# An FFN down-projection by seven block products instead of eight, placed between the next group's up tiles, with the block sums on the vector engine

## The chip, the cores and the metric

The kernel runs on one core of a Trainium2 chip. The metric is the device time of one execution in microseconds, the median of several runs. Engines are named as in the profile: PE is the matrix engine (TensorE) and PEld its weight loads, DVE the vector engine, ACT the scalar engine, POOL is GpSimd, SP the engine whose queue starts the DMAs here.

## The reference, cut to what matters

One decoder layer on 256 tokens of 2048 channels, all in float32. The part that the change touches is the FFN at its end:

```python
h = rmsnorm(x, g_ffn[l])
u = causal_dwconv(h @ w_up[l], ffn_conv_w[l]) + ffn_conv_b[l]
gate, val = jnp.split(u, 2, axis=-1)
x = x + (jax.nn.silu(gate) * val) @ w_down[l]
return rmsnorm(x, g_final)
```

`w_up` is 2048 x 11264 (5632 gate and 5632 value channels), `w_down` is 5632 x 2048. Ahead of it stand a mixing block (projections, a gated convolution, pooling, cross-attention, an output projection), which the change leaves alone.

## The kernel before

All large products are made on PE from float32 numbers that are split in two parts: `hi`, the number rounded to the float32r format by an ACT copy (L129), and `lo`, the rest, by a DVE subtraction (L130). A product a x w is then hi x hi + hi x lo + lo x hi, three matmuls where one would do.

The weights come as one stream of tiles of 1 MB, in a fixed order (`stream`, L103). `load` puts the DMA of a tile on SP's queue into one of three `raw` buffers; `split_tile` makes its `hi` and `lo`, 2048 columns wide, into three buffers each; `next_tile` hands the tile to the product that uses it, and first has the tile three further on loaded and the one two further on split. The order of instructions on each engine is set by a scheduler from the order of the code; each engine then works its queue strictly in that order.

The FFN works on units of 256 channels, 22 in all. A unit has four up tiles: two halves of the 2048 input channels for the gate, two for the value (`unit_a`, `mm_a`: 32 matmuls a tile, 16 of 512 and 16 of 256 columns). When the gate's or the value's two tiles are through, `up_finish` (L737) takes the result from PSUM: per 128 channels an ACT copy of the correction (L322), two DVE operations (L323 the sum, L324 the norm's factor), an ACT operation (L747) and two DVE multiply-adds (L751) for the convolution, and for the gate ACT's Silu (L755). At the end of a unit DVE multiplies gate and value (L776), and ACT and DVE split the product (L777, L778) into a group's activation tile `u`.

Units are taken in groups of 8, 7, 5 and 2. A group's down-projection (`down`, L782) comes after the first unit of the next group, and those of the last two groups after all units. It goes through the group's chunks of 128 channels in tiles of two chunks x 1024 columns (`mm_b`, L326): 24 matmuls of 512 columns a tile, accumulated over the group in four PSUM banks, which DVE at last adds into the residual `xt` (`add_in`, L706). The last group (`down_last`, L793) goes by pieces, with the final norm between them.

Of the kernel before, what the change touches and what calls it, by code (L numbers as in the profile page):

```python
# [12 lines left out]
ALU = mybir.AluOpType  # L13
# [11 lines left out]
def kernel(  # L25
# [45 lines left out]
    # Per-channel vectors, as columns of 128 channels, by transposing rows of 128.  # L71
# [20 lines left out]
    rows = lambda v: v.rearrange("(r c) -> r c", c=P)  # noqa: E731  # L92
# [10 lines left out]
    stream = []  # (source, nk, ncol, pieces)  # L103
# [4 lines left out]
    def load(i, between=None):  # L108
        src, nk, ncol, pieces = stream[i]
        raw = wpool.tile([P, nk, ncol], F32, tag="raw", name=f"raw_{i}")  # L110
# [23 lines left out]
    def split_tile(i):  # L134
        nk, pieces = stream[i][1], stream[i][3]
        step = nk // pieces
# [19 lines left out]
    n_units = NF // 2  # L156
    UNITS = [8, 7, n_units - 17, 2]  # sizes of FFN groups in units of 256 channels
# [20 lines left out]
    # The pool's weights: per pair of groups the three chunks' rows, in the columns of  # L178
    # the output chunks that they reach; wp_at[k] is the first of them.
# [17 lines left out]
    # Chunks of the mix in the order in which they come about.  # L197
# [10 lines left out]
    # A group's down-projection comes after the next group's first unit; that of the  # L208
    # last but one after all units.
    sched = []  # L210
    done = 0
    for gi, (a, n) in enumerate(group_of):
        upto = n_units if gi + 2 >= len(group_of) else a + n + 1
        for u in range(done, upto):
            sched.append(("up", u, [g for g, (b, m) in enumerate(group_of) if b <= u][-1]))
        done = upto
        sched.append(("down", gi, None))
    for what, a, b in sched:
        if what == "up" and a == 0:
            for h in (0, 1):  # L220
                plan_a(w_up, 0, (h,))
                plan_a(w_up, D_UP, (h,))
        elif what == "up":
            plan_a(w_up, a * 256)
            plan_a(w_up, D_UP + a * 256)
        else:
            a0, n = group_of[a]
            for n2 in range(2):
                plan_b(w_down, a0 * 2, n * 2, n2 * 1024, 1024, 2)

# [27 lines left out]
    def rstd_of(ssq, nm):  # L258
        """ssq [P, n] sums of squares -> 1 / sqrt(mean + eps), with a Newton step."""
# [14 lines left out]
    def row_of(r, nm):  # L274
        """[P, TB] per-token values -> the same row of S values in every partition."""
# [44 lines left out]
    def gather(ps, row, o, engine=nc.vector):  # L320
        """(main + corrections) * row -> o [P, S] in SBUF."""
# [4 lines left out]
    def mm_b(ps, wt, actT, ks, tbs, first, last):  # L326
        """ps[tb][n] += act[tokens of tb, chunk k] @ w[chunk k, columns of n]."""
# [41 lines left out]
    # The order of the first instructions is that in which the data arrive.  # L369
# [66 lines left out]
    def split_into(o, src, n=S):  # L436
        """float32 [P, n] -> o, its two parts one after the other."""
# [50 lines left out]
    # 1 / (number of tokens averaged) for the first tokens  # L488
# [73 lines left out]
    # The sums run on GpSimd while the next unit's products do; the rest comes after.  # L562
    pending = []

    def pool_sums(ps, i):
# [3 lines left out]
        spans = []  # (first row, last row, group) of this chunk  # L569
# [17 lines left out]
    def pool_means():  # L587
        for i, v, spans, sums in pending:
# [11 lines left out]
            # The convolution's chunks of the mix are free until it comes.  # L600
# [122 lines left out]
    row_2 = None  # L723
    u_tiles = {}

    def up_matmul(u):
        if u:
            return [unit_a(h2T, f"g{u}"), unit_a(h2T, f"v{u}")]
        ps = [[bank(f"pu0_{w}_{mi}") for mi in range(2)] for w in range(2)]
        for h in range(2):  # L730
            for w in range(2):
                mm_a(ps[w], next_tile(), h2T, h * 8, 8, h == 0, h == 1)
                if h == 0 and w == 0:
                    transpose_in(xt, h2T, "g_ffn", range(8, 16), "x2")
        return ps
# [190 lines left out]
```

## Time and profile before

| | |
|---|---|
| time, median of 3 runs | 1064.57 us (1064.54 to 1064.72) |
| the profiled execution: its span | 1064.7 us |
| PE busy | 1054.7 us (99%) |
| DVE busy | 703.6 us (66%) |
| ACT busy | 529.0 us (50%) |
| instructions on PE | 5632 matmuls, as many weight loads |
| instructions on DVE | 920 |
| mean granted clock of TensorE | 0.997 |
| read from memory | 198.99 MB, 189 GB/s |

The profiled execution's own time is its span, within 0.15 us of each of the three runs. A row of a group reads: line, engine, operation, output <- inputs with their sizes, count | busy us, mean ns of one | idle time of the engine before them and what ended it. A row of a timeline reads: start, length, engine, line and operation, count, and in brackets the idle time before it with what ended that. Lengths of neighbours on one engine can overlap. Matmuls are pipelined, so that a busy PE alone does not say that it is at its peak; the chain of waits is the better witness.

### The profile page before, as it was taken

Reading aid. Unit: us, or ns where it says so; the run is one execution under the profiler, and the core shown is the slowest. Engines: PE = TensorE matmul, PEld = TensorE weight load, DVE = VectorE, ACT = ScalarE, POOL = GpSimd, SP = SyncE. Lnnn points to the kernel's source line nnn. Section 1 sums busy time; section 2 is a strip of 40 time slices with the busy share of each in tenths; the row PEclk is TensorE's granted clock in tenths of the full one; section 3 lists DMA queues with packets and bytes.
Section 4 is the critical chain, followed back from the end, with each engine's and each line's share of the span. In section 5 each row is a group of like instructions: output and inputs, shape, how many; then the busy total and the mean of one; then the engine's idle time right before and its main releaser. Section 6 shows DMA issues by size and latency. Waiting matters only on the chain.

```text
span 1064.7 us, 14249 instructions
## 1 busy us (share of the span) xinstructions
PE 1054.7 (99%) x5632; PEld 907.2 (85%) x5632; DVE 703.6 (66%) x920; ACT 529.0 (50%) x683; POOL 43.1 (4%) x163
## 2 busy tenths in 40 slices
PE   9999999999999999999999999999999999999996
PEld 8888898888888888888888888888888888888885
DVE  5677786764556777777744467777754477777655
ACT  5965454443446655555533344554533345555343
POOL 0023500000000000000000000000000000000000
PEclk9999999999999999999999999999999999999998
DMA  9765465455555556555555555655555555654552
GB/s 316 243 224 172 143 206 189 161 195 183 186 185 174 184 196 198 188 181 185 198 198 198 196 171 187 198 185 175 195 198 197 191 174 190 198 177 178 198 198 80
DMA packets 147342, 202.01 MB, mean 190 GB/s; under 512 B 3619, under 2 KB 125771, under 8 KB 147147
## 3 DMA queue, kind: packets, MB, share of 16 engines
q1 hardware_dynamic: 147242, 201.09, 55.8%
q8 instruction: 44, 0.72, 0.3%
q14 instruction: 24, 0.19, 0.0%
q10 hardware_dynamic: 32, 0.01, 0.0%
HBM read 198.99 MB, written 2.10 MB: 189 GB/s over the span
## 4 chain that ended last, share of the span: by engine, by line
PE 98%; DVE 1%; ACT 0%; issue 0%; DVEq 0%
PE pa_v L306 15%; PE pa_g L306 15%; PE pa_g L309 7%; PE pa_v L309 7%; PE pd L338 7%; PE pd L344 7%; PE pd L341 7%; PE po L338 3%; PE po L341 3%; PE po L344 3%; PE pa_cc L306 2%; PE pa_cx L306 2%; PE pa_cb L306 2%; PE pa_pv L306 2%; PE pk L395 2%; PE pa_q L306 1%
## 5 line engine op out<-in xcount | busy, mean ns | idle before, releaser
L130 DVE TENSOR_TENSOR lo<-raw,hi 128x2048 fp32r<-128x2048 f32 (+2 forms) x196 | 425.5, 2172 | 271.6 <-ACT hi L129 270.6
L129 ACT ACTIVATE hi<-raw 128x2048 fp32r<-128x2048 f32 (+2 forms) x196 | 355.9, 1818 | 255.8 <-PE pd L344 98.4
L306 PE MATMUL pa_v<-h2T,hi 128*128 128x512 f32 x672 | 236.7, 396 | 0.0
L306 PE MATMUL pa_g<-h2T,hi 128*128 128x512 f32 x672 | 236.7, 396 | 0.0
L309 PE MATMUL pa_g<-h2T,lo 128*128 128x256 f32 x672 | 188.5, 281 | 0.0
L309 PE MATMUL pa_v<-h2T,lo 128*128 128x256 f32 x672 | 188.5, 281 | 0.0
L306 PEld LDWEIGHTS pa_v<-h2T,hi 128*128 128x128 f32 x672 | 126.0, 188 | 30.0
L306 PEld LDWEIGHTS pa_g<-h2T,hi 128*128 128x128 f32 x672 | 126.0, 188 | 30.0
L309 PEld LDWEIGHTS pa_g<-h2T,lo 128*128 128x128 f32 x672 | 127.0, 189 | 0.1
L309 PEld LDWEIGHTS pa_v<-h2T,lo 128*128 128x128 f32 x672 | 127.0, 189 | 0.0
L338 PE MATMUL pd<-hi,u 128*128 128x512 f32 x320 | 98.6, 389 | 0.0
L341 PE MATMUL pd<-lo,u 128*128 128x512 f32 x320 | 98.5, 389 | 0.0
L344 PE MATMUL pd<-hi,u 128*128 128x512 f32 x320 | 98.5, 389 | 0.0
L751 DVE SCALAR_TENSOR_TENSOR t<-h,cols,t 128x256 f32<-128x256 f32 x176 | 79.1, 480 | 2.2 <-ACT t L747 1.4
L755 ACT ACTIVATE t<-t 128x256 f32<-128x256 f32 x44 | 18.3, 418 | 107.0 <-DVE t L751 107.0
L341 PEld LDWEIGHTS pd<-lo,u 128*128 128x128 f32 x320 | 60.1, 188 | 12.6
L344 PEld LDWEIGHTS pd<-hi,u 128*128 128x128 f32 x320 | 60.1, 188 | 12.4
L338 PEld LDWEIGHTS pd<-hi,u 128*128 128x128 f32 x320 | 59.9, 188 | 12.4
L747 ACT ACTIVATE t<-h,cols 128x256 f32<-128x256 f32 x88 | 49.8, 593 | 0.0
L322 ACT ACTIVATE h<-pa_g 128x256 f32<-128x256 f32 x42 | 16.0, 380 | 61.3 <-PE pa_g L309 61.3
L338 PE MATMUL po<-hi,mixT 128*128 128x512 f32 x128 | 39.6, 391 | 0.0
L341 PE MATMUL po<-lo,mixT 128*128 128x512 f32 x128 | 39.5, 389 | 0.0
(207 smaller groups left out, 1280.9 us busy)
## 6 DMA issues: line engine op xcount, KB each, us to landing
raw<-in_w_up_dram SPq DMA_DIRECT2D x88, 1024.0 KB, 5.0
raw<-in_w_down_dram SPq DMA_DIRECT2D x44, 1024.0 KB, 4.9
raw<-in_w_in_dram SPq DMA_DIRECT2D x28, 1024.0 KB, 4.9
raw<-in_w_out_dram SPq DMA_DIRECT2D x16, 1024.0 KB, 4.9
raw<-in_w_kv_dram SPq DMA_DIRECT2D x4, 1024.0 KB, 5.2
raw<-in_w_kv_dram SPq DMA_DIRECT2D x6, 512.0 KB, 8.3
memt<-in_mem_dram SPq DMA_DIRECT2D x8, 256.0 KB, 7.7
xt<-in_x_dram SPq DMA_DIRECT2D x4, 512.0 KB, 6.7
```

The source lines that it names most:

```text
L129: nc.scalar.activation(hi[:, s, :], raw[:, s, :], AF.Copy)
L130: nc.vector.tensor_tensor(lo[:, s, :], raw[:, s, :], hi[:, s, :].bitcast(F32), op=ALU.subtract)
L306: nc.tensor.matmul(ps[mi], hi[:, kk, c], actT[:, k, :], start=first and kk == 0, stop=False)
L309: nc.tensor.matmul(ps[mi][:, S:], lo[:, kk, c], actT[:, k, :S], start=False, stop=last and kk == nk - 1,)
L322: nc.scalar.activation(o, ps[:, S:], AF.Copy)
L338: nc.tensor.matmul(ps[tb][n], ah, hi[:, kk, c], start=f, stop=False)
L341: nc.tensor.matmul(ps[tb][n], ah, lo[:, kk, c], start=False, stop=False)
L344: nc.tensor.matmul(ps[tb][n], al, hi[:, kk, c], start=False, stop=l)
L395: nc.tensor.matmul(psk[mi], wt[0][:, j, c], mT[:, k, :], start=k == 0, stop=False)
L747: nc.scalar.activation(t, hp[:, 2:], AF.Identity, bias=cvec("ffn_conv_b", m), scale=cw[2])
L751: nc.vector.scalar_tensor_tensor(t, hp[:, s : s + S], cw[s], t, op0=ALU.mult, op1=ALU.add)
L755: nc.scalar.activation(t, t, AF.Silu)
```

## The change

The groups are now five of 4 units and a last one of 2. For each of the five, the product of the group's activations A (256 tokens x 1024 channels) with its rows of `w_down` is made by a Strassen scheme (Winograd's order of the sums) for each half of the output columns (p = 0, 1: 1024 columns). A is cut in 2 x 2 blocks: token halves, and even and odd chunks of 128 channels; the rows and columns of `w_down` likewise, in blocks of 512 x 512 (b11, b12, b21, b22, 1 MB each). Seven products of blocks (12 matmuls of 512 columns each) take the place of eight. So two groups' worth of code is new:

- `turn` (L860 to L875), once a group, in place of the activation splits L777 and L778: DVE makes four sums of activation blocks, 512 wide, into a buffer of the `raw` pool, and ACT and DVE split these and three plain blocks into `sums` (seven left operands, hi and lo).
- `Blocks` loads the four weight blocks of a column half by SP's queue into three buffers (`rawd`, a part of the tile `ffn`) and splits the operand of each product (ACT L247, DVE L248, 2048 wide) as a tile of the stream. Between the products' splits DVE adds blocks in place (L240, 2048 wide), four times per column half: two after the first product's split, one after the second's, one after the fourth's. b21 is loaded into b12's buffer after the fourth split, the next half's blocks after the fifth to seventh.
- `prod` makes one product into one of three PSUM banks (a, b, c), two of which go on accumulating, and DVE adds or subtracts the bank into `xt` after each product (L903, 512 wide): 70 such adds in all.

The products go into the schedule between the up tiles of the next group: one after each tile from the fourth on, two after the last; in the last group (8 up tiles for 14 products) one after each of the first six, then two, then six in a row. The last group's own down-projection is made as before, but its activations go into the buffer of `h2T`. The core of the diff:

```diff
-    UNITS = [8, 7, n_units - 17, 2]  # sizes of FFN groups in units of 256 channels
+    UNITS = [4] * ((n_units - 2) // 4) + [2]
...
+        def split(self, i, idx):
+            raw = self.buf(("b11", "b11", "b11", "b12", "b22", "b21", "b11")[idx])
+            hi, lo = split[i] = [
+                wpool.tile([P, 4, 512], F32R, tag=t, name=f"{t}_{i}") for t in ("hi", "lo")
+            ]
+            nc.scalar.activation(hi, raw, AF.Copy)
+            nc.vector.tensor_tensor(lo, raw, hi.bitcast(F32), op=ALU.subtract)
+            if idx == 0:
+                self.add("b11", "b12")
+                self.add("b12", "b22")
+            elif idx == 1:
+                self.add("b11", "b22")
+            elif idx == 3:
+                self.load("b21")
+                self.add("b11", "b21")
+            elif self.next is not None and idx >= 4:
+                self.next.load({4: "b11", 5: "b22", 6: "b12"}[idx])
...
+        elif n == 4:
+            after = [0, 0, 0] + [1] * 12 + [2]
+        else:
+            after = [1, 1, 1, 1, 1, 1, 2, 6]
...
-            nc.vector.tensor_tensor(gates[mi], gates[mi], vals[mi], op=ALU.mult)
-            nc.scalar.activation(ut[:, c, :S], gates[mi], AF.Copy)
-            nc.vector.tensor_tensor(
-                ut[:, c, S:], gates[mi], ut[:, c, :S].bitcast(F32), op=ALU.subtract
-            )
...
-            for i in range(nk // 2):
-                mm_b(ps, next_tile(), ut, (2 * i, 2 * i + 1), range(TB), i == 0, i == nk // 2 - 1)
-            add_in(ps, n2 * 2, range(TB), f"d{gi}")
...
+        tt(t[:, 0], a21, a22, op=ALU.subtract)
+        tt(t[:, 2], a11, a21, op=ALU.subtract)
+        tt(t[:, 1], t[:, 0], a11, op=ALU.subtract)
...
+        tt(t[:, 3], t[:, 1], a12, op=ALU.add)
+        nc.scalar.activation(sums[:, 1:5, 0], t, AF.Copy)
...
+        tt(sums[:, 1:5, 1], t, sums[:, 1:5, 0].bitcast(F32), op=ALU.subtract)
...
+        for j in range(4):
+            ah, al = sums[:, i, 0, j, :], sums[:, i, 1, j, :]
+            for n, (a, b) in enumerate(((ah, hi), (ah, lo), (al, hi))):
+                nc.tensor.matmul(
+                    ps, a, b[:, j, :], start=first and j == 0 and n == 0,
+                    stop=j == 3 and n == 2, skip_group_check=True,
+                )
+        c0 = bl.p * 1024 + right * 512
+        o = xt[:, tb, c0 : c0 + 512]
+        nc.vector.tensor_tensor(o, o, ps, op=op)
```

Two places on DVE's queue. First, before, around the end of a unit (unit 13; `h` is a half unit's result, `t` its convolved form, `lo_127` and `lo_128` splits of stream tiles 127 and 128, `u` the group's activations):

```order
L324 TENSOR_TENSOR h_13_1_1_6161<-h_13_1_1_6161,row_x2_3031 128x256
L130 TENSOR_TENSOR lo_127_6181<-raw_127_6114,hi_127_6180 128x2048
L751 SCALAR_TENSOR_TENSOR t_13_1_0_6157<-h_13_1_0_6152,cols_86,t_13_1_0_6157 128x256
L751 SCALAR_TENSOR_TENSOR t_13_1_1_6166<-h_13_1_1_6161,cols_86,t_13_1_1_6166 128x256
L751 SCALAR_TENSOR_TENSOR t_13_1_0_6157<-h_13_1_0_6152,cols_86,t_13_1_0_6157 128x256
L751 SCALAR_TENSOR_TENSOR t_13_1_1_6166<-h_13_1_1_6161,cols_86,t_13_1_1_6166 128x256
L776 TENSOR_TENSOR t_13_0_0_6059<-t_13_0_0_6059,t_13_1_0_6157 128x256
L776 TENSOR_TENSOR t_13_0_1_6069<-t_13_0_1_6069,t_13_1_1_6166 128x256
L130 TENSOR_TENSOR lo_128_6219<-raw_128_6178,hi_128_6218 128x2048
L778 TENSOR_TENSOR u_1_4479<-t_13_0_0_6059,u_1_4479 128x256
L778 TENSOR_TENSOR u_1_4479<-t_13_0_1_6069,u_1_4479 128x256
```

And now, at the end of unit 12, the first of a group, after the turn; tiles 135 and 137 are products (`pp`), 136 is an up tile, `ffn` holds the weight blocks and the unsplit activations:

```order
L389 TENSOR_TENSOR h_12_1_1_5977<-h_12_1_1_5977,row_x2_2997 128x256
L248 TENSOR_TENSOR lo_135_5991<-ffn_2826,hi_135_5990 128x2048
L812 SCALAR_TENSOR_TENSOR t_12_1_0_5973<-h_12_1_0_5968,cols_86,t_12_1_0_5973 128x256
L812 SCALAR_TENSOR_TENSOR t_12_1_1_5982<-h_12_1_1_5977,cols_86,t_12_1_1_5982 128x256
L812 SCALAR_TENSOR_TENSOR t_12_1_0_5973<-h_12_1_0_5968,cols_86,t_12_1_0_5973 128x256
L812 SCALAR_TENSOR_TENSOR t_12_1_1_5982<-h_12_1_1_5977,cols_86,t_12_1_1_5982 128x256
L844 TENSOR_TENSOR ffn_2826<-t_12_0_0_5875,t_12_1_0_5973 128x256
L844 TENSOR_TENSOR ffn_2826<-t_12_0_1_5885,t_12_1_1_5982 128x256
L240 TENSOR_TENSOR ffn_2826<-ffn_2826 128x2048
L903 TENSOR_TENSOR xt_90<-xt_90,pp_4_a_5995 128x512
L132 TENSOR_TENSOR lo_136_6012<-raw_136_5988,hi_136_6011 128x2048
L248 TENSOR_TENSOR lo_137_6050<-ffn_2826,hi_137_6049 128x2048
```

Where two 2048 wide splits stood in this stretch, there are now three and a block sum of the same width, with an add into `xt`. Second, the last down-projection before the final one, on DVE's queue (`pd` are its PSUM banks), before:

```order
L130 TENSOR_TENSOR lo_178_8379<-raw_178_8338,hi_178_8378 128x2048
L130 TENSOR_TENSOR lo_179_8409<-raw_179_8376,hi_179_8408 128x2048
L130 TENSOR_TENSOR lo_180_8439<-raw_180_8406,hi_180_8438 128x2048
L130 TENSOR_TENSOR lo_181_8469<-raw_181_8436,hi_181_8468 128x2048
L130 TENSOR_TENSOR lo_182_8499<-raw_182_8466,hi_182_8498 128x2048
L706 TENSOR_TENSOR xt_90<-pd_2_1_0_0_8372,xt_90 128x512
L706 TENSOR_TENSOR xt_90<-pd_2_1_0_1_8373,xt_90 128x512
L706 TENSOR_TENSOR xt_90<-pd_2_1_1_0_8374,xt_90 128x512
L706 TENSOR_TENSOR xt_90<-pd_2_1_1_1_8375,xt_90 128x512
L130 TENSOR_TENSOR lo_183_8544<-raw_183_8496,hi_183_8543 128x2048
```

And now, the last products in a row (tiles 206 to 210; `h2T` takes the last group's activations; 211 is the final down-projection's first tile):

```order
L248 TENSOR_TENSOR lo_207_8454<-ffn_2826,hi_207_8453 128x2048
L504 TENSOR_TENSOR h2T_2275<-t_21_0_0_8277,h2T_2275 128x256
L504 TENSOR_TENSOR h2T_2275<-t_21_0_1_8287,h2T_2275 128x256
L248 TENSOR_TENSOR lo_208_8474<-ffn_2826,hi_208_8473 128x2048
L903 TENSOR_TENSOR xt_90<-xt_90,pp_9_a_8375 128x512
L240 TENSOR_TENSOR ffn_2826<-ffn_2826 128x2048
L248 TENSOR_TENSOR lo_209_8491<-ffn_2826,hi_209_8490 128x2048
L903 TENSOR_TENSOR xt_90<-xt_90,pp_9_a_8375 128x512
L248 TENSOR_TENSOR lo_210_8510<-ffn_2826,hi_210_8509 128x2048
L903 TENSOR_TENSOR xt_90<-xt_90,pp_9_b_8459 128x512
L132 TENSOR_TENSOR lo_211_8529<-raw_211_8507,hi_211_8528 128x2048
L903 TENSOR_TENSOR xt_90<-xt_90,pp_9_c_8532 128x512
```

A split per tile with one round of adds for the whole column half has become a split, an add into `xt` and in places a sum for each product, and the add of product 206 (the first row of `pp_9_a`) stands behind the split of 208. That bank goes on accumulating in product 207.

More of the change, by code (lines that the diff above doesn't have):

```diff
@@ L210 @@
+    blocks = []
+    for gi in range(len(group_of) - 1):
+        for p in range(2):
+            blocks.append(Blocks(len(blocks), gi, p))
+            if len(blocks) > 1:
+                blocks[-2].next = blocks[-1]
     sched = []
-    done = 0
+    prods = []
     for gi, (a, n) in enumerate(group_of):
[L213 to L217, printed above, removed]
@@ L218 @@
-    for what, a, b in sched:
[L219 to L229, printed above, removed]
+        n_t = 4 * n
+        if not prods:
+            after = [0] * n_t
+        elif n == 4:
+            after = [0, 0, 0] + [1] * 12 + [2]
+        else:
+            after = [1, 1, 1, 1, 1, 1, 2, 6]
@@ new lines @@
+        assert sum(after) == len(prods)
+        for t in range(n_t):
+            sched.append(("up", a + t // 4, t % 4))
+            for _ in range(after[t]):
+                sched.append(prods.pop(0))
+        if gi < len(group_of) - 1:
+            sched.append(("turn", gi, None))
+            prods = [("prod", b, i) for b in blocks[2 * gi : 2 * gi + 2] for i in range(N_PROD)]
+    for what, a, b in sched:
+        if what == "up":
+            w, h = (b % 2, b // 2) if a == 0 else (b // 2, b % 2)
+            plan_a(w_up, w * D_UP + a * 256, (h,))
+        elif what == "prod":
+            stream.append((a, None, b, 1))
```

127 lines of the change are left out of this document (90 added, 37 removed).

## The prediction

> **What bounds the kernel now.** I read the page first (busy times and the chain that ended last), then what TensorE itself waited for.
>
> ```profile
> span 1064.7 us, 14249 instructions
> PE 1054.7 (99%) x5632; PEld 907.2 (85%) x5632; DVE 703.6 (66%) x920; ACT 529.0 (50%) x683; POOL 43.1 (4%) x163
> ...
> PE 98%; DVE 1%; ACT 0%; issue 0%; DVEq 0%
> ...
> PE warm L67 <- DVE ones L58: 1.0, 1, 1.0
> PE pk L395 <- DVE mT L249: 0.3, 1, 0.3
> ```
>
> The last two rows are all the waits of PE (engine, line, waited for: us in total, times, longest): 1.3 us, both in the first microseconds. From there to the last product PE never starves, so fewer matmuls is a direct gain, as long as PE still never starves. The others have room, as the busy times of the FFN show (five stretches from 321 to the end at 1064.7, summed), and the vector engine's timeline while down-projection tiles pass (start, length, engine, line, and in brackets the idle time before):
>
> ```profile
> sum 743.70, PE 734.98 PEld 631.76 DVE 495.11 ACT 361.10 POOL 9.20; mean PE 147.00 PEld 126.35 DVE 99.02 ACT 72.22 POOL 1.84
> ...
> 535.23 2.29 DVE L130 TENSOR_TENSOR lo<-raw,hi 128x2048 fp32r<-128x2048 f32 x1 [2.47 <-ACT hi L129]
> 540.66 2.29 DVE L130 TENSOR_TENSOR lo<-raw,hi 128x2048 fp32r<-128x2048 f32 x1 [3.15 <-ACT hi L129]
> 546.05 2.29 DVE L130 TENSOR_TENSOR lo<-raw,hi 128x2048 fp32r<-128x2048 f32 x1 [3.10 <-ACT hi L129]
> ```
>
> DVE works 495 of 744 us (67%). In the down-projection it does one 2.29 us split per tile and then idles about 3.1 us. That idle time is what the change spends.
>
> **What the change removes.** The three matmul groups of the down-projection, and their pace on the chain:
>
> ```profile
> L338 PE MATMUL pd<-hi,u 128*128 128x512 f32 x320 | 98.6, 389 | 0.0
> L341 PE MATMUL pd<-lo,u 128*128 128x512 f32 x320 | 98.5, 389 | 0.0
> L344 PE MATMUL pd<-hi,u 128*128 128x512 f32 x320 | 98.5, 389 | 0.0
> ...
> 525.02 0.45 PE pd L338 x2
> ...
> 526.38 0.45 PE pd L338 x2
> ```
>
> Six matmuls take 526.38 - 525.02 = 1.36 us, so 0.227 us each. Groups 0 to 2 of before have 40 chunks x 24 = 960 of them; the change has 10 column halves x 7 products x 12 = 840. The 120 fewer are worth 120 x 0.227 = **27.2 us**, all on PE's path. A product takes 12 x 0.227 = 2.72 us. For an up tile I take a quarter of a unit's period (first row to last, below: 422.59 - 400.41 = 22.18), 5.55 us.
>
> **What it adds, and the price of each row.** Instructions of DVE overlap a little, so I price them from start to next start:
>
> ```profile
> 400.41 0.42 DVE L323 TENSOR_TENSOR h<-pa_g,h 128x256 f32<-128x256 f32 x1 [0.83 <-ACT h L322]
> 400.87 0.43 DVE L324 TENSOR_TENSOR h<-h,row_x 128x256 f32<-128x256 f32 x1
> ...
> 411.89 0.76 DVE L323 TENSOR_TENSOR h<-pa_v,h 128x256 f32<-128x256 f32 x2 [0.76 <-ACT h L322]
> 412.56 0.75 DVE L324 TENSOR_TENSOR h<-h,row_x 128x256 f32<-128x256 f32 x2
> 413.96 2.29 DVE L130 TENSOR_TENSOR lo<-raw,hi 128x2048 fp32r<-128x2048 f32 x1 [0.65 <-ACT hi L129]
> 416.18 1.67 DVE L751 SCALAR_TENSOR_TENSOR t<-h,cols,t 128x256 f32<-128x256 f32 x4
> 417.76 0.75 DVE L776 TENSOR_TENSOR t<-t,t 128x256 f32<-128x256 f32 x2
> ...
> 422.59 0.42 DVE L323 TENSOR_TENSOR h<-pa_g,h 128x256 f32<-128x256 f32 x1 [0.83 <-ACT h L322]
> ...
> 319.26 2.48 DVE L706 TENSOR_TENSOR xt<-po,xt 128x512 f32<-128x512 f32 x4
> ...
> L706 DVE TENSOR_TENSOR xt<-pd,xt 128x512 f32<-128x512 f32 x24 | 14.9, 683 | 0.0
> ...
> 399.99 0.39 ACT L322 ACTIVATE h<-pa_g 128x256 f32<-128x256 f32 x1 [2.79 <-PE pa_g L309]
> 400.27 1.91 ACT L129 ACTIVATE hi<-raw 128x2048 fp32r<-128x2048 f32 x1
> 402.08 0.59 ACT L747 ACTIVATE t<-h,cols 128x256 f32<-128x256 f32 x1
> ```
>
> So: 2048 wide 2.21 (413.96 to 416.18); 512 wide 0.60 ((2.48 - 0.683) / 3); 256 wide 0.335 (two in 0.67), 0.13 more when it needs the row right before (400.41 to 400.87); a multiply-add of L751 0.40 (four in 1.58). ACT's 2048 wide copy takes 1.81 (400.27 to 402.08), its PSUM copy 0.39.
>
> The block sum has no row in this trace. It is the same instruction and width as the split, f32 instead of fp32r out. The nearest row is the split itself, so I take 2.21. The upper end is its full length, 2.29. The lower end is what 256 more columns cost between a 256 and a 512 wide row, 0.60 - 0.335 = 0.265, eight times: 2.12. For all 40 sums that is 3.6 us less or 3.2 more.
>
> Over the FFN, DVE loses 40 tile splits and gains 70 product splits, 40 block sums and 5 wide splits in the turns: 75 x 2.21 = 166 us. It gains 46 adds into the residual and 35 rows of 512 in the turns (81 x 0.60 = 49 us) and loses 40 of L778's (13 us). That is 202 us more: 495 + 202 = 697 us of work in 744 - 27 = 717, from 67% to 97%. In the steady part, a group of 16 up tiles and 14 products, PE needs 16 x 5.55 + 14 x 2.72 = 126.9 us. DVE has 16 + 14 splits, 8 sums and one wide split of the turn (39 x 2.21 = 86.2), 32 multiply-adds (12.8), 40 rows of 256 (13.4) and 21 of 512 (12.6): 125.0. A queue worked in order at 98% loses wherever the load is uneven, and it is very uneven: sums and turn stand close together.
>
> **Where PE then starves.** I followed the queues of DVE, ACT and PE row by row at these prices. A tile's number is its place in the stream, as in the order's lo_136. A stall has a floor, DVE's rows between two events that PE sets, all back to back, and a value from the walk, which adds DVE's waits for ACT.
>
> The turn. DVE cannot start on the last half unit before tile 126 ends on PE. From there to lo_136 it has 12 wide rows (26.5), 10 of 512 (6.0), 12 multiply-adds (4.8) and 16 of 256 (5.4): 42.7, with 0.39 for ACT's copy and 0.13, 43.2 us. PE has in that time products 127, 128, 133, 135 (10.9), up tiles 129 to 132 and 134 (27.7) and three early matmuls (0.7): 39.3. It stalls 3.9 us at least. In the walk 2.0 more: lo_129 waits 1.1 for hi_129, which ACT makes only after the copy (0.39 + 1.81), and the turn's parts 0.9 for ACT. In us after tile 126, DVE ends: lo_129 4.5, lo_130 9.1, the turn's sums 15.8, lo_131 18.0 (PE wants it at 16.5), the wide split 20.2, lo_132 22.4, lo_133 26.0, a block sum 29.9, lo_134 32.1, a sum 34.3, lo_135 37.9, a sum 42.4, lo_136 45.2, where PE without a stall is at 39.3. So 5.9, three times: 17.7 (floor 11.7). The first turn has no products before it: floor 0.2, walk 4.4, since ACT's copy of hi_74, behind tile 71 on PE, stands ahead of the L747 that DVE needs.
>
> The second column half of a group. From the end of tile 114 to lo_118 DVE has four wide rows, two of them sums: 12.9 us against 12.1 on PE, floor 0.8; the walk waits 1.1 for hi_117 and loses 0.7 again at tile 122: 2.6, four times: 10.4 (floor 3.2).
>
> The last group. Here the products follow a single up tile, and the last six stand in a row. Tile 186 to lo_195: DVE 38.0, PE 30.25, floor 7.7 (walk 9.1). Tile 199 to lo_206: 25.6 against 22.0, 3.6 (4.7). Then 207 waits for the add of 206, which stands behind lo_208: 8.0 against 2.95, 5.0. Product 209 waits 1.1 in the walk, for its sum. Together 16.3, walk 20.0.
>
> Each product's add into xt waits for PE on DVE's queue, and the next split stands behind it; in the walk DVE is late there and the product has long ended, so these 70 waits cost nothing, and where DVE is early they cost nothing either, since two split tiles lie ahead of PE.
>
> Other edits come at nothing. ACT does 30 more copies of 1.81, 54 us; a steady part has 30 of them (54), 16 PSUM copies (6) and 16 L747 (0.59, 9) in 127 us of PE's work, which hides them, but for the places where one stands ahead of another as told above. The bytes of w_down stay: forty 1 MB block loads for forty tiles. One lands in
>
> ```profile
> raw<-in_w_down_dram SPq DMA_DIRECT2D x44, 1024.0 KB, 4.9
> ```
>
> 4.9 us. The block loaded during a product's half (b21) is issued when its buffer's split ends, and DVE has 5.1 us of rows before the sum that needs it: covered by 0.2 us, else up to 1 us for each of ten. On SP's queue a block load stands ahead of some up tiles; those are loaded three tiles, about 16 us, before they are split, which covers it.
>
> Sum: 1064.7 - 27.2 + 4.4 + 17.7 + 10.4 + 20.0 = **1090.0 us**. With all stalls at the floor (0.2 + 11.7 + 3.2 + 16.3 = 31.4) it is 1068.9. I take the walk, as ACT's queue order is fixed. The profiled span is 0.1 us above the median of the runs, 1064.57, so it needs no correction.
>
> **Rivals.**
> *TensorE's clock falls in the stalls.* The tail of before shows it (window; then after the busy times the granted clock):
>
> ```profile
> 1054.00:1057.00 3.00, 1.98 (x17) 1.78 (x15) 2.96 (x8) 1.61 (x6) 0.00 (x0) 1.00 0.54 208
> 1057.00:1060.00 3.00, 0.00 (x0) 0.00 (x0) 2.62 (x8) 0.35 (x3) 0.00 (x0) 0.75 0.48 180
> 1060.00:1064.70 4.70, 0.00 (x0) 0.00 (x0) 1.04 (x2) 0.00 (x0) 0.00 (x0) 0.50 0.52 199
> ```
>
> PE's last matmul ends at about 1056.0, and 0.75 over 1057 to 1060 means half speed from about 1058.5: 2.5 us after. Seven stalls (four at turns, three in the last group) are longer than that. If half speed then lasts as long as the idle time that brings it, 2.5 us, each costs 1.25 us: 9 us, 1099. Against it: some of those stalls are broken by single matmuls, and a slower PE gives DVE time to catch up. The Trainium skill, "TensorE: Matmul & The Clock Gate", part 1, says that the clock halves after an idle window of about 3.4 us and comes back after as long a busy one; the tail agrees on the half, at 2.5 us. By that rule each drop would cost 1.7 us (an estimate from that page), and the time would be 1102.
>
> *DVE keeps ahead (faster).* Its total, 125.0, does fit into PE's 126.9, and three buffers of hi and lo lie between the two. If DVE did its wide rows in 1.88 us instead of 2.21, the twelve of a turn would save 3.9 us and the floor there would be zero; that is the point from which it decides. Then turns and second halves cost nothing, only the last group's 16.3 is left: 1064.7 - 27.2 + 16.3 = 1053.8. For it speaks that the sum in place has no row here, and that PE's order already sets early matmuls where a split is late. Against it, every 2048 wide row of DVE takes 2.29.
>
> *It cancels out.* Between: stalls of about 27 us, 1064.7, if ACT's waits vanish and a floor or two is too high.
>
> **How the numbers follow.** The forecast (1069 to 1096) has 0.64, the clock 0.16, DVE ahead 0.12, cancelling 0.04, and 0.04 is for something worse than 1106. A measurement of this kernel can tell about 0.2%, 2.1 us, from no change. Slower takes 0.64 + 0.16 + 0.04 = 0.84, same 0.04, faster 0.12. The range reaches from 1066 (the floor sum, with the 40 sums at their lower price) to 1106, above the clock's case; it leaves out DVE ahead and the worst, about 0.16 to 0.18. Predicted: 1090.
>
> **What would show it.** Right: PE with 120 matmuls fewer and waits for DVE's lo of 30 to 60 us in all, in bunches of 3 to 6 us after each turn and at the six last products; DVE at 93% or more of the FFN; block sums of 2.2 to 2.3 us. Wrong: PE waiting under 27 us; sums that take under 1.9 us; PE's waits put down to DMA, which would mean that the loads of blocks are late. A granted clock under 1.0 between the turns would show the rival on the clock.

## The result and the profile after

| | before | after |
|---|---|---|
| time, median of the runs | 1064.64 us (4 runs, 1064.54 to 1066.4) | 1095.30 us (4 runs, 1093.63 to 1096.81) |
| ratio to before | | 1.0285 (95% interval 1.027 to 1.030) |
| profiled execution: time, span | 1066.4, 1064.7 us | 1094.7, 1092.9 us |

The change makes the kernel 2.9% slower; the forecast was 1090. One thing in the table corrects the prediction at once. The time is 1.8 us above the span in both kernels. Of before the profiled execution took 1.8 us more than the other runs, so its span happened to equal their median. Span is therefore set against span here: 1064.7 and 1092.9, 28.2 us. The four runs of after differ with the mean granted clock of TensorE: 1093.63 and 1094.72 us at 0.987, 1095.88 and 1096.81 at 0.981.

From the page of after: span, busy times, the chain that ended last, and the group of the block sums with its waits.

```profile
span 1092.9 us, 14170 instructions
PE 1044.2 (96%) x5512; PEld 887.5 (81%) x5512; DVE 895.4 (82%) x1036; ACT 593.0 (54%) x693; POOL 43.0 (4%) x163
...
PE 74%; DVE 14%; ACT 4%; issue 4%; DMA 2%; DVEq 0%; ACTq 0%; SPq 0%
...
L240 DVE TENSOR_TENSOR ffn<-ffn 128x2048 f32<-128x2048 f32 x40 | 91.4, 2286 | 8.7 <-DMA ffn<-in_w_down_dram 8.7
...
ffn<-in_w_down_dram SPq DMA_DIRECT2D x40, 1024.0 KB, 6.2
```

PE was 98% of the chain and is now 74%; 14% has gone to DVE. A block sum takes 2.29 us, the length of a split. PE's waits in the FFN (engine, line, waited for: us in total, times, longest):

```profile
PE pp_a L897 <- ACT hi L247: 17.1, 6, 3.7
PE pu L371 <- ACT hi L131: 5.6, 4, 1.4
PE pp_a L897 <- DVE sums L870: 5.4, 1, 5.4
PE pp_b L897 <- ACT hi L247: 3.2, 3, 1.5
PE pp_a L897 <- DVE lo L248: 2.0, 1, 2.0
PE pp_b L897 <- DVE lo L248: 1.8, 1, 1.8
PE pp_c L897 <- DVE lo L248: 1.5, 1, 1.5
...
PE pu L374 <- DVE lo L132: 1.0, 4, 0.3
```

That is 37.6 us, where before had none. Most of it stands beside ACT's `hi`, and the row misleads a reader who stops there. One matmul of product 137 is queued ahead of tile 136 and needs only `hi_137`. ACT makes `hi_137` as soon as DVE's block sum is done, so the matmul is released 0.7 us before `lo_136`, for which PE would have waited anyway. DVE's timeline around the third turn shows this (start, length, engine, line); the PE rows below it are the moment at which tile 126 ends and product 127 starts, and the end of the wait.

```profile
680.70 2.29 DVE L132 TENSOR_TENSOR lo<-raw,hi 128x2048 fp32r<-128x2048 f32 x1 [0.92 <-ACT hi L131]
...
685.30 2.28 DVE L132 TENSOR_TENSOR lo<-raw,hi 128x2048 fp32r<-128x2048 f32 x1
...
693.44 2.28 DVE L132 TENSOR_TENSOR lo<-raw,hi 128x2048 fp32r<-128x2048 f32 x1
695.64 2.29 DVE L875 TENSOR_TENSOR sums<-turn,sums 128x2048 fp32r<-128x2048 f32 x1
...
701.38 2.29 DVE L248 TENSOR_TENSOR lo<-ffn,hi 128x2048 fp32r<-128x2048 f32 x1
...
705.40 2.29 DVE L240 TENSOR_TENSOR ffn<-ffn 128x2048 f32<-128x2048 f32 x1
707.61 2.29 DVE L132 TENSOR_TENSOR lo<-raw,hi 128x2048 fp32r<-128x2048 f32 x1
...
717.80 2.29 DVE L240 TENSOR_TENSOR ffn<-ffn 128x2048 f32<-128x2048 f32 x1
...
720.60 2.29 DVE L132 TENSOR_TENSOR lo<-raw,hi 128x2048 fp32r<-128x2048 f32 x1
```

```profile
678.57 0.40 PE L897 MATMUL pp_c<-hi,sums 128*128 128x512 f32 x1
...
722.17 0.50 PE L897 MATMUL pp_a<-hi,sums 128*128 128x512 f32 x1 [3.71 <-ACT hi L247]
722.94 0.80 PE L374 MATMUL pu<-h2T,lo 128*128 128x256 f32 x2 [0.27 <-DVE lo L132]
```

DVE's rows stand edge to edge, about 2.2 us from start to start, and PE waits 3.7 us and 0.3 more, until the last of them is done. The six places at which TensorE's granted clock fell (window; then the busy times of PE, PEld, DVE, ACT and POOL; then the granted clock):

```profile
449.00:453.00 4.00, 3.72 (x13) 3.10 (x13) 4.00 (x4) 1.40 (x1) 0.00 (x0) 0.57 0.61 190
586.00:590.00 4.00, 3.89 (x12) 3.05 (x13) 4.00 (x4) 1.86 (x2) 0.00 (x0) 0.57 0.49 150
722.00:727.00 5.00, 4.56 (x17) 3.72 (x17) 5.00 (x4) 1.92 (x2) 0.00 (x0) 0.66 0.59 193
859.00:863.00 4.00, 3.84 (x13) 3.38 (x14) 4.00 (x4) 1.13 (x1) 0.00 (x0) 0.57 0.69 217
968.00:972.00 4.00, 3.09 (x8) 2.48 (x9) 4.00 (x6) 1.91 (x1) 0.00 (x0) 0.57 0.00 0
1040.00:1047.00 7.00, 5.49 (x12) 3.80 (x12) 7.00 (x11) 3.71 (x4) 0.00 (x0) 0.51 0.05 7
```

Each lies right behind one of the longest stalls. Work done at a granted clock of 0.57 loses 0.43 of its time, so the rows give 1.60 + 1.67 + 1.55 + 1.65 + 1.33 + 2.69 = 10.5 us. The account of the span, each stall taken from the gaps between PE's starts (0.15 to 0.3 us more per wait than the list of waits counts, since matmuls overlap); the first up matmul starts at 320.3 us in before and at 318.6 in after, and what stands ahead of it is the part that the change leaves alone:

| us | predicted | measured |
|---|---|---|
| before | 1064.7 | 1064.7 |
| 120 matmuls fewer | -27.2 | -27.2 (taken over) |
| first turn | 4.4 | 5.7 |
| three turns | 17.7 | 14.3 |
| four second halves | 10.4 | 6.3 |
| last group | 20.0 | 16.6 |
| half clock | a rival's | 10.5 |
| earlier start of the FFN | 0 | -1.7 |
| not placed by these | 0 | 3.7 |
| sum | 1090.0 | 1092.9 |

Of the 3.7 us some 1.6 are the products' own matmuls: their starts are 0.229 us apart on average where nothing stalls, against 0.227 in the down-projection of before. The rest stays open.

### The profile page after: what moved, and what is told of

It reads as the page before. It is cut to its first block, busy times and chain, and to the rows that moved or that the text cites. A ratio compares the mean times of both kernels' runs of the same rounds, so it can differ in the third digit from the quotient of the medians.

```text
span 1092.9 us, 14170 instructions
## 1 busy us (share of the span) xinstructions
PE 1044.2 (96%) x5512; PEld 887.5 (81%) x5512; DVE 895.4 (82%) x1036; ACT 593.0 (54%) x693; POOL 43.0 (4%) x163
## 4 chain that ended last, share of the span: by engine, by line
PE 74%; DVE 14%; ACT 4%; issue 4%; DMA 2%; DVEq 0%; ACTq 0%; SPq 0%
PE pu L371 23%; PE pu L374 12%; PE pp_a L897 5%; DVE ffn L240 4%; PE pp_b L897 3%; DVE lo L132 3%; PE po L406 3%; PE po L403 3%; PE po L409 3%; DVE t L812 2%; PE pa_cx L371 2%; PE pa_cc L371 2%; PE pa_cb L371 2%; PE pa_pv L371 2%; DVE lo L248 2%
## 5 line engine op out<-in xcount | busy, mean ns | idle before, releaser
L371 PE MATMUL pu<-h2T,hi 128*128 128x512 f32 x1408 | 499.1, 399 | 5.6 <-ACT hi L131 5.6
L132 DVE TENSOR_TENSOR lo<-raw,hi 128x2048 fp32r<-128x2048 f32 (+3 forms) x156 | 333.2, 2138 | 97.2 <-ACT hi L131 96.3
L374 PE MATMUL pu<-h2T,lo 128*128 128x256 f32 x1408 | 394.2, 283 | 1.2 <-DVE lo L132 1.0
L131 ACT ACTIVATE hi<-raw 128x2048 fp32r<-128x2048 f32 (+3 forms) x156 | 279.1, 1792 | 103.9 <-PE po L409 39.3
L371 PEld LDWEIGHTS pu<-h2T,hi 128*128 128x128 f32 x1408 | 266.0, 190 | 68.6 <-ACT hi L131 7.3
L374 PEld LDWEIGHTS pu<-h2T,lo 128*128 128x128 f32 x1408 | 267.4, 191 | 7.8 <-DVE lo L132 5.8
L247 ACT ACTIVATE hi<-ffn 128x2048 fp32r<-128x2048 f32 x70 | 133.9, 1914 | 80.8 <-DVE ffn L240 34.3
L248 DVE TENSOR_TENSOR lo<-ffn,hi 128x2048 fp32r<-128x2048 f32 x70 | 160.1, 2287 | 13.6 <-ACT hi L247 13.5
L897 PE MATMUL pp_a<-hi,sums 128*128 128x512 f32 x320 | 109.1, 403 | 22.6 <-ACT hi L247 17.1
L240 DVE TENSOR_TENSOR ffn<-ffn 128x2048 f32<-128x2048 f32 x40 | 91.4, 2286 | 8.7 <-DMA ffn<-in_w_down_dram 8.7
L897 PEld LDWEIGHTS pp_b<-hi,sums 128*128 128x128 f32 x160 | 30.2, 189 | 11.3 <-ACT hi L247 5.0
```

The lines of the kernel that those rows point to most:

```text
L131: nc.scalar.activation(hi[:, s, :], raw[:, s, :], AF.Copy)
L132: nc.vector.tensor_tensor(lo[:, s, :], raw[:, s, :], hi[:, s, :].bitcast(F32), op=ALU.subtract)
L240: nc.vector.tensor_tensor(self.buf(to), self.buf(to), self.buf(what), op=ALU.add)
L247: nc.scalar.activation(hi, raw, AF.Copy)
L248: nc.vector.tensor_tensor(lo, raw, hi.bitcast(F32), op=ALU.subtract)
L371: nc.tensor.matmul(ps[mi], hi[:, kk, c], actT[:, k, :], start=first and kk == 0, stop=False)
```

## The experiments

The theory (A): VectorE's queue decides, because the work of the seven products stands too densely there at the turns, in the second halves and in the last group, and the half clock follows from its stalls. Its rivals: ScalarE's copies, which the waits name (B), late loads of blocks (C), and the order itself, products between up tiles (D). Times are medians, ratios are to before with their 95% interval, measured on the same chip.

**No block sums.**

```diff
 def add(self, to, what):
-    nc.vector.tensor_tensor(self.buf(to), self.buf(to), self.buf(what), op=ALU.add)
+    pass
```

> Leaves out the 40 block sums of VectorE (the products then use the wrong blocks); all else, TensorE's 5512 matmuls and ScalarE's 70 copies of products too, stays. Theory A, VectorE's queue decides: it loses 40 x 2.21 = 88 us. From tile 126 to lo_136 it then has 43.2 - 3 x 2.21 = 36.6 us against TensorE's 39.3, in a second half 12.9 - 2 x 2.21 = 8.5 against 12.1, so those stalls go and the half clock behind them. What stays is the first product of the last group, which waits 5.4 us for the turn's sums and not for a block sum, with 1.7 us of half clock, and 3 to 6 us of odd waits: 1064.7 - 27.2 + 7.1 + 3 to 6 = 1048 to 1051, in any case under 1056. Rival B, the row that names TensorE's waits is right and ScalarE's copy hi is late by its own queue: ScalarE has the same copies in the same order, so the 17.1 us of such waits and their clock stay, 1080 to 1090. Rival C, the block loads (6.2 us to land, 8.7 us of waits in after) are late: the splits wait instead of the sums, 1070 to 1085. Rival D, the order with products between up tiles costs by itself: above 1064.

Measured: 1050.38 us, ratio 0.9863 (0.9848 to 0.9878), 44.9 us below after. PE's waits in the FFN, but for two of 0.2 us:

```profile
PE pp_b L897 <- DVE lo L248: 2.8, 1, 2.8
PE pp_b L897 <- ACT h2T L503: 1.3, 1, 1.3
...
PE pp_b L897 <- DVE sums L875: 0.4, 1, 0.4
```

ScalarE has the same copies in the same order, and yet its `hi` is no longer waited for anywhere: rival B is out. Rival C and D would have kept the time above 1064 and are out too. The time is A's, but one detail is not: the 5.4 us wait for the last turn's sums went down to 0.4 as well, and 2.8 us at the last products stayed, with 2.8 us of half clock behind them.

**Stalls filled with matmuls that add zero.**

```diff
+def idle(ps, n):
+    for _ in range(n):
+        nc.tensor.matmul(ps, zero, h2T[:, 8, :], start=False, stop=False, skip_group_check=True)
 ...
+if i == 1:
+    idle(ps, n)
```

> Adds 103 matmuls with a zero left operand (0.227 us each), which add nothing to the accumulator: 16 behind the second product of each of the first four groups' first half, 22 behind the first up tile of the last group, 17 behind the second product of the last half, each just ahead of a wait of TensorE that the trace of after shows (3.7, 3.7, 3.7, 3.7, 5.4 us, and 1.8 + 2.0). The waits themselves are VectorE's and end when they did. Theory A with the clock: in after the granted clock is 0.5 for about 3.4 us behind each of these places, 10.7 us of TensorE's busy time lost in all. With TensorE busy there the clock stays at 1.00 and the time falls by 7 to 11 us, to 1084 to 1088. Rival, the half clock is hidden, because VectorE is behind there anyway and gets as much time back as TensorE loses: no change within 2 us, 1093 to 1097. If the filling comes at a wrong moment, up to 103 x 0.227 = 23 us more.

Measured: 1090.99 us, ratio 1.0245 (1.023 to 1.026), 4.3 us below after. The windows of the first turn and of the last products:

```profile
449.00:453.00 4.00, 3.67 (x19) 2.64 (x18) 4.00 (x3) 2.77 (x2) 0.00 (x0) 1.00 0.22 60
...
1040.00:1050.00 10.00, 5.33 (x17) 3.89 (x16) 7.77 (x7) 2.04 (x2) 0.00 (x0) 0.83 0.36 105
```

The half clock is gone at all five turns and stays, shorter, among the last products, where a new wait of 3.0 us for an add into `xt` came up. What is left of it is one stretch of 3.4 us with 3.0 us of matmuls, which lose half of that, 1.5. So of 10.5 us of lost busy time 9.0 came back, and the kernel gained 4.3. Neither expectation holds whole: as far as this one run shows, about half of what the clock costs TensorE is time that VectorE uses to catch up. With PE hardly idle at the turns and the clock at 1.00, the kernel is still 26 us slower than before, so the clock follows the stalls and is not the main cost.

**Eight plain products between the up tiles.** Four blocks for a column half, each split once and used for both halves of the tokens (24 matmuls); the turn only splits `u`.

```diff
-N_PROD = 7
+N_PROD = 4
-after = [0, 0, 0] + [1] * 12 + [2]
+after = [0, 0, 0, 1, 0, 1, 1, 0, 1, 0, 1, 1, 0, 1, 0, 1]
```

> The same groups of four units, the same blocks of w_down in the same three buffers, products between the next group's up tiles, but eight plain block products for a column half in place of seven (four blocks, each split once and used for both halves of the tokens), no block sums, and a turn that only splits u. The result is the reference's. TensorE has the 5632 matmuls of before. Theory A, the load that the seven products put on VectorE is the cost and the order is not: VectorE's work is about that of before, TensorE waits little, 1064 to 1069. Rival D, the order of products between up tiles, the turn or the loads of blocks cost by themselves: 1075 or more. The difference to after is then the price of the seven products alone.

Measured: 1069.06 us, ratio 1.0041 (1.0026 to 1.0055). In the FFN PE waits once, in the final projection:

```profile
PE pl L388 <- DVE h2T L483: 1.0, 1, 1.0
```

The order costs 4.4 us over before. This wait is 1.0 of them; by the starts of the matmuls, the products' take 0.229 us each and not 0.227 (about 1.7 us for 960), and a pair of up matmuls 0.3515 and not 0.3507 on average (about 1.2 us for 1408). The seven products alone cost 1095.3 - 1069.1 = 26.2 us. D is out as the main cause; these are fewer and longer products than after's, and the run without sums, which keeps after's order, rules it out as well.

**The block sums on GpSimd.** Besides, the sum of b12 and b22 stands behind the second product's split here.

```diff
-nc.vector.tensor_tensor(self.buf(to), self.buf(to), self.buf(what), op=ALU.add)
+nc.gpsimd.tensor_tensor(self.buf(to), self.buf(to), self.buf(what), op=ALU.add)
```

> The 40 block sums on GpSimd instead of VectorE, the sum of b11 and b22 ahead of that of b12 and b22; the result is the reference's. A 256 wide tensor_tensor of GpSimd takes 0.62 to 1.24 us in this trace, so a 2048 wide one 5 to 10 us (eight times). Theory A: VectorE loses 88 us of work. If a sum takes 5 to 6 us, sum and split of a product (about 10 us) are a little longer than up tile and product of TensorE (8.4), two tiles of lead take that up, and it gives 1045 to 1060. If a sum takes 8 to 10 us, TensorE waits 4 to 6 us for each of the first two sums of a half, ten halves: 1085 to 1120. Rival, the two engines hinder each other when both read SBUF: VectorE's 2048 wide rows get longer than 2.29 us beside a sum, and the time stays at 1085 or above even with short sums. ScalarE's order deciding (rival B): no gain, 1090 or above.

Measured: 1165.06 us, ratio 1.0941 (1.0925 to 1.0957). GpSimd's group of sums, then its timeline and VectorE's at the same moments:

```profile
L240 POOL TENSOR_TENSOR ffn<-ffn 128x2048 f32<-128x2048 f32 x40 | 210.0, 5249 | 233.4 <-DVE lo L248 130.1 <-DMA ffn<-in_w_down_dram 102.8 <-POOL h L804 0.3
```

```profile
430.60 4.79 POOL L240 TENSOR_TENSOR ffn<-ffn 128x2048 f32<-128x2048 f32 x1 [14.14 <-DVE lo L248]
...
436.72 6.39 POOL L240 TENSOR_TENSOR ffn<-ffn 128x2048 f32<-128x2048 f32 x1
```

```profile
430.43 6.03 DVE L812 SCALAR_TENSOR_TENSOR t<-h,cols,t 128x256 f32<-128x256 f32 x4
436.38 2.28 DVE L132 TENSOR_TENSOR lo<-raw,hi 128x2048 fp32r<-128x2048 f32 x1
...
439.25 4.48 DVE L389 TENSOR_TENSOR h<-h,row_x 128x256 f32<-128x256 f32 x2
```

The rival with the mutual hindrance is right, and it is all or nothing. Four multiply-adds take 1.67 us elsewhere and 6.03 here: they stop while the sum runs and end after it. The second sum in turn waits for the split that began before it (6.39 against 4.79 us). VectorE's busy time is 957.1 us, against 813.9 with no sums at all: a sum on GpSimd takes 143 / 40 = 3.6 us from VectorE, more than the 2.2 it took there. The Trainium skill, "SBUF — State Buffer", "Who interferes with whom", says that a VectorE instruction with two SBUF inputs contends with a GpSimd instruction that reads SBUF, and of the ports that the two share that "it's an exclusive lock". These rows agree.

**One sum later.** The total stays, one of the three sums moves out of the dense place.

```diff
 if idx == 0:
     self.add("b11", "b12")
-    self.add("b12", "b22")
 elif idx == 1:
     self.add("b11", "b22")
+elif idx == 2:
+    self.add("b12", "b22")
```

> One change to after: the sum of b12 and b22 goes on VectorE's queue behind the split of the third product, not the first (it is needed by the fourth). The result is the reference's, and VectorE's total work is the same. Theory A, the loss is the unevenness: from tile 126 to lo_136 VectorE has 43.2 - 2.2 = 41.0 us, so each of the five turns loses 2.2 us of stall, the rest of a stall is too short for the half clock (about half of whose cost counts, as the filled stalls showed: 4.3 of 9.3 us), and in the four second halves 10.7 us stand against 12.1, so the 1.5 us there go. 5 x 2.2 + 4 x 1.5 + 3 to 4 = 20 us less than after: 1073 to 1078. Rival, VectorE's total (125 of 128 us in a group) is the bound and the sum only moves the wait: under 6 us less, 1089 or above.

Measured: 1080.42 us, ratio 1.0149 (1.0127 to 1.0171), 14.9 us below after. Some of PE's waits:

```profile
PE pu L375 <- DVE lo L132: 9.3, 11, 1.7
PE pp_a L898 <- ACT hi L247: 7.0, 5, 1.6
PE pp_b L898 <- DVE xt L904: 4.0, 1, 4.0
```

Each of the first four turns lost the expected 2.1 to 2.2 us of stall (the 3.7 us wait is now 1.5 to 1.6), and the half clock left all turns but the first. The second halves kept their 1.5 us, at a later tile, and the last group got worse (4.0 us for an add). I had expected 20 us and got 14.9: unevenness is real, and it is not all.

**The last group plain.** As above, and the down-projection among the last group's two units by plain block products (for each group and column half, S is seven products and P plain ones).

```diff
+KINDS = ("SS", "SS", "SS", "SS", "PP")
-after = [1, 1, 1, 1, 1, 1, 2, 6]
+after = [0, 1, 1, 1, 1, 1, 1, 2]
```

> The late sum, and besides the down-projection that stands among the last group's two units as eight plain block products for a column half instead of seven (no sums, no turn sums there). The result is the reference's. TensorE has 24 matmuls more than after, 5.5 us. Theory A: in after the last group alone waits some 18 us and runs 4.7 us of its work at half clock; with plain products VectorE has 6 splits and 8 sums less there, 31 us, and those waits go: 18 + 2 to 4 - 5.5 = 15 us below the late sum alone: 1058 to 1063, slightly faster than before. Rival, the last group's waits come from the order (one up tile between turn and first product, products in a row) and not from VectorE's work: less than 8 us below the late sum alone.

Measured: 1069.15 us, ratio 1.0040 (1.0025 to 1.0055), 11.3 us below the late sum. PE waits nowhere in the last group now, where by the gaps it had lost 17.9 us; against 5.5 us for 24 more matmuls that is a gain of 12.4. I had expected 15, with the half clock of that place; but the clock now fell at three turns where it had not with the late sum alone:

```profile
446.00:450.00 4.00, 3.27 (x17) 2.64 (x18) 4.00 (x3) 2.21 (x2) 0.00 (x0) 1.00 0.42 116
570.00:576.00 6.00, 4.78 (x18) 4.17 (x19) 6.00 (x9) 3.95 (x4) 0.00 (x0) 0.72 0.54 175
714.00:720.00 6.00, 5.66 (x22) 4.69 (x23) 6.00 (x5) 1.82 (x2) 0.00 (x0) 0.72 0.52 175
848.00:854.00 6.00, 5.55 (x22) 4.59 (x23) 6.00 (x5) 1.93 (x2) 0.00 (x0) 0.72 0.55 175
```

**Seven products in the second halves only.** First halves and the last group plain.

```diff
+KINDS = ("PS", "PS", "PS", "PS", "PP")
+after = [0, 0, 1, 0, 1, 0, 1, 0, 1, 1, 1, 1, 1, 0, 1, 2]
```

> Seven products only in the second column half of the first four groups; the first halves and the last group with plain block products. The result is the reference's. TensorE saves 4 x 12 = 48 matmuls against the plain products everywhere (1069.1 us): 10.9 us. VectorE has 33 wide rows in a group in place of 39, so it should keep ahead of TensorE everywhere: theory A 1069 - 10.9 + 0 to 3 = 1058 to 1061. Rival, a place with three to four wide rows in a row still stalls TensorE in each second half by 3 us or more: above 1066.

Measured: 1060.32 us, ratio 0.9955 (0.9939 to 0.9972): faster than both kernels, and 8.7 us below plain products everywhere. PE's only waits in the FFN:

```profile
PE pu L386 <- DVE lo L132: 1.1, 4, 0.3
```

Here 48 matmuls fewer are worth most of their 10.9 us, since VectorE has room: 586.6 of 739.0 us of the FFN, 79%.

**No loads of b21.**

```diff
 elif idx == 3:
-    self.load("b21")
     self.add("b11", "b21")
```

> After without the ten loads of b21 (1 MB each); the sixth product and the last sum use the old sum of b12 and b22 in that buffer, so the result is not the reference's. In after VectorE waits 8.7 us for these loads, six times. Theory A, VectorE has time there, so only what falls ahead of a stall counts: 1 to 3 us less, 1092 to 1094. Rival C, the late loads push VectorE's queue and with it all later stalls: 7 to 9 us less, 1086 to 1088.

Measured: 1096.0 us, ratio 1.0294 (1.0279 to 1.0309), no less than after. The 8.7 us for which VectorE waits for these loads went down to 0.8 and bought nothing: it had that time. The clock does not hide a gain: at a mean of 0.981 two of these runs took 1096.4 and 1098.0 us, two of after's 1095.9 and 1096.8. C is out by itself.

**Products one up tile later.** One line of the kernel with the last group plain.

```diff
-after = [0, 0, 0] + [1] * 12 + [2]
+after = [0, 0, 0, 0] + [1] * 10 + [2, 2]
```

> One change to the kernel with the late sum and the plain last group (1069.2 us): in the four groups of sevens the fourteen products start one up tile later and two of the last three pairs of up tiles carry two products (0, 0, 0, 0, ten times 1, 2, 2). The result is the reference's. Theory A, the loss is where work stands and not how much of it there is: an up tile gives VectorE about 1.8 us (5.65 on TensorE, 3.8 on VectorE), so of the 2.1 to 2.6 us that TensorE still waits at each turn 1.8 go, and with them the half clock at two of them (5.0 us of busy time, about half of it counts): 4 x 1.8 + 2.5 = 9.7 us less, 1058 to 1062. Rival, the total is the bound (125 of 128 us): the wait comes back where two products follow one up tile or at the second half, 1066 to 1072.

Measured: 1070.69 us, ratio 1.0056 (1.0041 to 1.0072), no gain. All of PE's waits in the FFN:

```profile
PE pu L386 <- DVE lo L132: 12.9, 13, 1.8
PE pu L383 <- ACT hi L131: 5.2, 4, 1.3
```

The wait of 1.5 to 2.1 us at the turn fell to 0.2 to 0.6 us and came back two tiles later (1.7 to 1.8), in the second half (1.3) and behind the sixth product (1.0 to 1.1). The rival is right: with 125 us of VectorE's work for 128 of TensorE's, a stall that is ordered away at one place shows at the next. The clock stayed at 1.00 and the time did not fall.

**Seven products in the last group's second half too.**

```diff
-KINDS = ("PS", "PS", "PS", "PS", "PP")
+KINDS = ("PS", "PS", "PS", "PS", "PS")
```

> One more half to the kernel with seven products in the second halves only (1060.3 us): the last group's second half by seven products too, so 60 matmuls fewer than with plain products. The result is the reference's. TensorE has 12 x 0.227 = 2.7 us less. Seven products beside three to four up tiles cost VectorE 7 x (4.07 - 2.73) - 4 x 1.8 = 2.2 us more than TensorE takes, which two tiles of lead (8 us) hold: theory A 1057 to 1059. Rival, the products in a row at the end of the last group wait for their sums as in after: 1062 to 1068.

Measured: 1063.58 us, ratio 0.9989 (0.998 to 0.9997). The rival's case: 2.7 us of matmuls are saved and about 5 us of waits come for them by the gaps, 1.6 of it at a sum among the last products and 1.4 in the final projection, whose split stands behind theirs.

## Why the prediction was right, point by point

- *The gain of 27.2 us* is there but for a few: with waits and half clock taken off, the span of after is 1092.9 - 42.9 - 10.5 = 1039.5, against 1037.5 forecast, and its FFN began 1.7 us earlier. So up to 3.7 us are missing, 1.6 of them by the products' 0.229 us per matmul.
- *The price of a block sum*, 2.21 (2.12 to 2.29): 2.21 from start to start (705.40 to 707.61). (With the sums at 2.12 the floor sum is 1065.3; the range's lower end says 1066.)
- *The walk at the turn* was right row by row. In us after tile 126, walk and trace: lo_129 4.5 and 4.4, lo_130 9.1 and 9.0, lo_131 18.0 and 17.2, wide split 20.2 and 19.4, lo_133 26.0 and 25.1, sum 29.9 and 29.1, lo_135 37.9 and 37.1, sum 42.4 and 41.5, lo_136 45.2 and 44.3. The 0.9 us are the turn's waits for ScalarE, which did not occur. The stall was 4.4 to 5.5 us in place of 5.9: the 0.9, and an up tile that takes 5.62 to 5.65 us there and not 5.55, which brings PE later to the same place.
- *The first turn*: 5.7 measured, 4.4 predicted. It is like the others; the floor of 0.2 was the wrong end.
- *The second halves*: 1.6 each, between floor 0.8 and walk 2.6. *The last group*: 16.6, its floor (16.3) and not the walk (20.0); 5.4 of it stood at its first product, which waits for the turn's sums. The total agrees better than its parts.
- *VectorE's load*: 686 us in the FFN against 697 predicted. Its share was to be 93% or more. It is 93% in the four-unit groups (126.4 of 136 us) and 89% over all, since the span grew and the last part has room. *Waits of 30 to 60 us* for VectorE: 37.6, with the rows that name ACT read as above.
- *Adds into xt*: that VectorE waits for PE there cost nothing, as said. The one add for which PE was to wait, product 206's for 207, did hold it, though the list names `lo_208` for it, since one matmul of product 208 is queued ahead:

```profile
1048.22 0.68 DVE L903 TENSOR_TENSOR xt<-xt,pp_a 128x512 f32<-128x512 f32 x1
```

```profile
1048.36 0.50 PE L897 MATMUL pp_b<-lo,sums 128*128 128x512 f32 x1 [1.84 <-DVE lo L248]
1048.96 0.50 PE L897 MATMUL pp_a<-hi,sums 128*128 128x512 f32 x1
```

  Product 207 starts at 1048.96, as the add ends (1048.90). VectorE's stretch from `lo_206` to there is 7.9 us (8.0 forecast), but PE stalls 2.6 us by the gaps and not 5.0: product 206 ran at half clock (11 matmuls in 4.86 us, where 0.227 each make 2.50). VectorE's rows stand edge to edge through it, so in this place the half clock cost nothing. In two experiments another product's add, that of bank b, was waited for by name (3.0 and 4.0 us).
- *The b21 load is covered, else up to 1 us each*: block loads landed in 6.2 us (median) and not 4.9 and VectorE waited, but without it the time is the same.
- *The clock* was put as a rival of 9 to 12 us instead of the forecast. It came in addition: six drops, 10.5 us of TensorE's time. The prediction's own argument against it, that a slower PE gives VectorE time, held for about half, as the filled stalls showed (4.3 of 9.0). The stalls came out 9.6 us smaller than forecast and the clock cost 10.5 that the sum did not have; they nearly cancel, and that 1090.0 lies only 2.9 us from 1092.9 is luck. The path and the cause were right, the sum was closer than its terms.
- *VectorE keeps ahead* and *it cancels out* fell: the point on which the first hung, wide rows of 1.88 us, was not reached.

## What to carry to other kernels

One product less saves TensorE 2.7 us for a column half here and costs VectorE seven wide rows more (three splits, four sums; 15.5 us): such a trade pays only up to the point where the other engine's queue, counted stage by stage, still has some room, here 79% of the FFN and not 125 of 128 us in a group. A part of it, four of ten column halves (1060.3 us), beat both all of it (1095.3) and none (1064.7). Where a queue is that full, moving work about moves the wait about; take work out, and read behind a wait's name what the named engine itself had waited for.

## What the runs showed of the hardware

- The half clock lasts a whole number of stretches of 3.4 us: (1 - 0.57) x 2 x 4 us = 3.4 us in the windows of after, 6.9 in the last. What brings it on is not a fixed idle time. In the kernel with the last group plain, waits of 2.10, 1.57 and 1.50 us brought it at three turns, and one of 1.55 us at the first turn did not. The Trainium skill, "TensorE: Matmul & The Clock Gate", "What's actually happening", says of the clock that activity is watched in a free-running window of about 3.4 us. The traces agree. Narrower windows put the six falls of after at 449.54, 586.08, 722.61, 859.14, 968.37 and 1040.05 us; they are 136.53, 136.53, 136.53, 109.23 and 71.68 us apart, which is 40, 40, 40, 32 and 21 times 3.413 us, while the four turns' waits end at other distances (137.5, 136.1 and 136.2 us). What counts is how long PE is idle within one step of that grid. The steps at the four turns of the kernel with the last group plain, of which the last three end with a fall (PE's busy time is the first number behind the comma):

```profile
442.85:446.26 3.41, 2.06 (x10) 1.36 (x8) 3.41 (x3) 1.76 (x1) 0.00 (x0) 1.00 0.01 2
569.14:572.55 3.41, 1.33 (x8) 1.23 (x9) 3.41 (x6) 3.29 (x2) 0.00 (x0) 1.00 0.01 3
712.50:715.91 3.41, 1.57 (x9) 1.16 (x9) 3.41 (x3) 3.32 (x2) 0.00 (x0) 1.00 0.00 0
845.63:849.04 3.41, 1.64 (x7) 0.82 (x5) 3.41 (x4) 2.82 (x2) 0.00 (x0) 1.00 0.00 0
```

  At the first turn a step ends while PE still waits, so the idle time is shared by two steps. In all kernels here a step at full clock with under 1.75 us of idle PE never ended with a fall, one with over 1.9 always did. So the same stall can bring the half clock or not, by where it lies on the grid.
- The pace of up tiles changes within a kernel. In before, a pair of their matmuls takes 0.347 us up to the first down-projection at about 525 us (17 pairs in 5.89 us from 439.94) and 0.353 after it (18 in 6.36 from 699.62). But it is not the down-projection that brings it: in the kernel with filled stalls a pair takes 0.354 before any product (16 in 5.66 us from 380.26), and in after the pace goes back to 0.348 for a while behind a stall (9 in 3.13 us from 726.07). Over all up tiles, where nothing stalls, the pair takes 0.351 us in before and in after alike, so none of what the account leaves open is due to it. The cause is open.
- A 2048 wide addition of GpSimd takes 4.8 us where nothing holds it up, and stops VectorE's instructions with two SBUF inputs for as long.
